# The depthwise convolution's fourth feature block goes from 16 to 31 taps on the tensor engine

## The chip, the cores and the metric

The kernel runs on one core of a Trainium2 chip. What counts is the device time of one execution in microseconds (us), the median of several runs. The engines are told by the profile's names: PE (tensor engine, matmul), PEld (its weight loads), DVE (vector engine), ACT (scalar engine), POOL (GpSimd), SP (the engine whose queue issues the weight loads from memory).

## The reference, cut to what matters

The program is two small networks one after the other on 256 tokens of 1024 features. The first network's second layer has a mixer with a depthwise convolution of 31 taps over 768 features, and that alone is touched here:

```python
def odd_mixer(y, w_in, conv_w, conv_b, cnorm_g, pool_w, pool_scale, w_out):
    z = y @ w_in
    ga, gb, q = jnp.split(z, [D_CONV, 2 * D_CONV], axis=-1)
    u = ga * jax.nn.sigmoid(gb)
    u = lax.conv_general_dilated(u, conv_w[:, None, :], window_strides=(1,),
                                 padding=[(CONV_WIDTH // 2, CONV_WIDTH // 2)],
                                 dimension_numbers=('NWC', 'WIO', 'NWC'),
                                 feature_group_count=D_CONV) + conv_b
    u = jax.nn.silu(rmsnorm(u, cnorm_g))
    ...
    return jnp.concatenate([u, p], axis=-1) @ w_out
```

Around it stand gated feed-forward layers (`half_ffn`: gate and up products into 2816 features, then a down product back), each ahead of and behind the mixer.

## The kernel before

Activations lie with features on the 128 partitions and the 256 tokens along the row. Every large product is made of three half-precision matmuls for each 128x128 tile of weights (`mm3`: high part by high part, high by low, low by high), which PE works through at one 128x256 matmul in about 0.11 us.

**The weights.** Each weight unit (up to 128 x 2048 values) is loaded by SP's queue into one of three staging buffers (`_load`, L122), then split into a high and a low half-precision tile: ACT writes the high part (L137) and DVE the low part (L138), 1024 columns at a time. There are four split buffers, and a unit is split when PE has done with an older one. A staging buffer comes free when DVE has split it, and only then is the next load issued.

**The feed-forward layer ahead of the mixer** (`half_ffn(W, 1, 0, 3, ...)` in `middle`) ends with its down product in `project`: four blocks of 256 features, each of three weight units (8, 8 and 6 tiles of 128 rows). After each block `accumulate` updates the two row blocks of the residual on DVE (L1226), squares them on ACT into one of two buffers of the tag `sq` (L323), and POOL adds the squares together (L311). Ahead of the last block stands a small product on an unsplit weight unit that is read straight from its staging buffer (`early`, matmuls `m<-stage,craw`); that unit is the first of the mixer, `in_o_w_in`.

**The convolution** works on six blocks of 128 features. `CONV` gives for each block the number of taps done by PE, and the engine of the rest: block 0 has all taps on ACT (products, L1390) and POOL (sums, L1391), blocks 1 and 2 all taps on DVE (L1383 for the first, L1385 for the rest), block 3 has 16 taps on PE and 15 on DVE, and blocks 4 and 5 have all 31 on PE. A tap on PE is three matmuls against diagonal 128x128 matrices. `taps`, called between the two feed-forward layers, has POOL build these matrices in advance, two for each tap (high and low part), each with one instruction (L1299). In the program's text they stand ahead of the whole feed-forward layer in whose time they are built.

**After the convolution** `odd` squares the six results on ACT in the order of `ORDER` and sums them over the partitions with a matmul by ones (`m<-sq,ones`), takes the reciprocal root (L333, L334), scales and applies silu (`prep`, L1401, L1402), and feeds the output product `part`. The parts of that product that don't depend on the convolution (kt 6 and 7, the pooling branch) are queued ahead. The next layer's early product (`before`, again `m<-stage,craw`, then a product on POOL in place, L444, and a copy on DVE, L442) stands between.

The order of instructions on each engine is set when the program is built: of the instructions that its own estimate holds to be ready, the one that stands first in the program's text goes first. On the chip each engine then runs its list strictly in that order.

```python
            for i in range(2):
                for k in range(n):
                    nc.gpsimd.tensor_scalar(diag[f][:, i, k], id16, w[:, i, k : k + 1], None, op0=OP.mult)
...
            if n == 31:
                nc.scalar.activation(acc[f], bc[f][:, :S], AF.Identity, scale=ISW, bias=self.v("o_conv_b", f, 1))
...
            if n:
                nc.vector.scalar_tensor_tensor(acc[f], bc[f][:, :S], ISW, acc[f], op0=OP.mult, op1=OP.add)
        add = self.summed(stat[:, :S], direct=6, n=6, ones=ones)
        for f in self.ORDER:
            add(self.square(acc[f], S))
```

Of the kernel before, what the change touches and what calls it, by code (L numbers as in the profile page):

```python
# [215 lines left out]
class Program:  # L216
# [1055 lines left out]
        return rst  # L1272


    CONV = ((0, "gpsimd"), (0, "vector"), (0, "vector"), (16, "vector"), (31, None), (31, None))
    ORDER = (0, 1, 4, 3, 2, 5)

    def taps(self, op, cr):

# [8 lines left out]
        diag = {}  # L1288
        for f, (n, _) in enumerate(self.CONV):
            if n == 0:  # L1290
# [11 lines left out]
    def odd(self, W, y, rst, op, taps):  # L1302
# [18 lines left out]
        for f in range(6):  # L1321
# [15 lines left out]
            nc.vector.scalar_tensor_tensor(up[:, f, 15 : 15 + S], bk[:, :S], ISW, sg, op0=OP.mult, op1=OP.mult)  # L1337
            if self.CONV[f][0]:
                us[f] = t([P, S + 30], f"uh{f}", F16), t([P, S + 30], f"ul{f}", F16)
# [10 lines left out]
        def conv(f, bank):  # L1350
            n = self.CONV[f][0]
            bc[f] = self.bank(bank)
            for k in range(n):
                self.mm3(bc[f][:, :S], diag[f][:, 0, k], diag[f][:, 1, k], us[f][0][:, k : k + S], us[f][1][:, k : k + S], k == 0, k == n - 1)
            if n == 31:
                nc.scalar.activation(acc[f], bc[f][:, :S], AF.Identity, scale=ISW, bias=self.v("o_conv_b", f, 1))
# [21 lines left out]
        nextu = self.before(W, 1, 6, 5)  # L1378
        for f, (n, eng) in enumerate(self.CONV):
            if n == 31:  # L1380
# [13 lines left out]
# [3 lines that stand above are left out]
# [510 lines left out]
```

## Time and profile before

| what | us |
|---|---|
| median of 3 runs | 2735.67 (2726.55 to 2736.68) |
| the profiled execution | 2735.91 |
| its span in the trace | 2734.1 |
| PE busy in the span | 2619.9 (96%) |
| DVE busy in the span | 1749.9 (64%) |

The profiled execution took 1.8 us more than its span; that lies around the span and isn't seen in the trace. Times in the rows below are microseconds from the span's start. In a timeline a row is one or several like instructions: start, length, engine, line, operation, output<-inputs with their shapes, and in brackets how long the engine stood idle before it and what it then waited for.

### The profile page before, as it was taken

How to read it: one execution, taken by the hardware profiler on the slowest of the kernel's cores; microseconds unless marked ns; L12 is line 12 of the kernel's file. 1: busy time of each engine (PE TensorE's matmuls, PEld its weight loads, DVE VectorE, ACT ScalarE, POOL GpSimd, SP SyncE). 2: the span in 40 equal slices, each digit the busy share in tenths (PEclk: the TensorE clock that was granted, in tenths of full speed). 3: DMA queues.
4: the chain of work that ended last, by engine and by line, in shares of the span. 5: the costliest groups of instructions: out<-in, count | busy, mean ns of one | idle time of the engine just before them, and what ended most of it. 6: DMA issues, size and time to landing. Idle time of an engine off the chain costs nothing.

```text
span 2734.1 us, 53369 instructions
## 1 busy us (share of the span) xinstructions
PE 2619.9 (96%) x23012; PEld 2009.6 (74%) x23012; DVE 1749.9 (64%) x2601; ACT 1278.9 (47%) x1821; POOL 423.5 (15%) x413
## 2 busy tenths in 40 slices
PE   8999998799999899999989999999999999999998
PEld 4444444476667678888878887888888888888887
DVE  6676676765567366665676556666565666766664
ACT  5454555443344254444645445554544455544443
POOL 0000010321121000199520010000120300000301
PEclk9999999988798899999999999999999999999999
DMA  9676784100102156655626666555656655556563
GB/s 313 240 254 229 263 291 134 53 27 21 32 14 74 40 171 193 208 184 192 182 79 201 193 194 194 169 177 165 214 170 193 200 163 166 171 157 222 170 193 101
DMA packets 427775, 451.71 MB, mean 165 GB/s; under 512 B 9890, under 2 KB 414920, under 8 KB 420243
## 3 DMA queue, kind: packets, MB, share of 16 engines
q1 hardware_dynamic: 422272, 441.29, 50.7%
q10 hardware_dynamic: 5267, 7.01, 0.8%
q8 instruction: 180, 2.95, 0.5%
q14 instruction: 56, 0.46, 0.1%
HBM read 447.18 MB, written 1.08 MB: 164 GB/s over the span
## 4 chain that ended last, share of the span: by engine, by line
PE 60%; DVE 8%; issue 4%; ACT 4%; DMA 2%; POOL 2%; ACTq 0%; SPq 0%; POOLq 0%; DVEq 0%
PE g L232 48%; PE w L232 4%; PE m L232 4%; DVE w L138 3%; PE n L232 2%; ACT w L137 2%; PE m L235 1%; DVE acc L1385 1%; DMA stage<-in_w_in 1%; DVE SC L1057 1%; POOL acc L1391 0%; DMA stage<-in_o_w_in 0%; PE o L232 0%; DVE yl L347 0%; DVE xn L484 0%
## 5 line engine op out<-in xcount | busy, mean ns | idle before, releaser
L232 PEld LDWEIGHTS <-w 128*128 128x128 f16 x14784 | 1440.5, 98 | 447.2 <-issue 96.9
L138 DVE SCALAR_TENSOR_TENSOR w<-stage,w 128x1024 f16<-128x1024 f32 (+2 forms) x812 | 971.6, 1230 | 455.5 <-ACT w L137 453.2
L137 ACT ACTIVATE w<-stage 128x1024 f16<-128x1024 f32 (+2 forms) x812 | 797.7, 1031 | 542.2 <-PE g L232 317.4
L232 PE MATMUL g<-yh,w 128*128 128x256 f16 x5568 | 931.1, 273 | 8.4 <-ACT yh L346 8.3
L232 PE MATMUL g<-yl,w 128*128 128x256 f16 x2784 | 759.1, 273 | 5.6 <-DVE yl L347 5.1
L232 PE MATMUL g<-hh,w 128*128 128x256 f16 (+1 forms) x1936 | 343.0, 282 | 0.0
L232 PE MATMUL g<-hl,w 128*128 128x256 f16 (+1 forms) x968 | 273.4, 282 | 0.0
L232 PE MATMUL g<-y0h,w 128*128 128x512 f16 (+1 forms) x704 | 219.2, 380 | 8.8 <-ACT y0h L346 8.5
L1299 POOL TENSOR_SCALAR diag<-ident,cws 128x128 f16<-128x128 f16 x156 | 144.2, 943 | 8.9 <-DVE cws L1294 8.9
L232 PE MATMUL g<-w,yh 128*128 128x256 f16 (+1 forms) x928 | 138.1, 262 | 0.2 <-ACT ak L1633 0.2
L232 PE MATMUL g<-y0l,w 128*128 128x512 f16 (+1 forms) x352 | 133.8, 381 | 1.3 <-DVE y0l L347 1.3
L232 PE MATMUL g<-w,yl 128*128 128x256 f16 (+1 forms) x464 | 116.5, 262 | 0.0
L311 POOL TENSOR_TENSOR acc<-sq,sq 128x256 f32<-128x256 f32 (+1 forms) x9 | 11.7, 1295 | 625.4 <-ACT sq L753 338.5
L232 PE MATMUL n<-y0h,w 128*128 128x512 f16 x352 | 108.2, 379 | 0.0
L514 ACT ACTIVATE silu<-g 128x512 f32<-128x512 f32 x50 | 29.9, 597 | 155.9 <-issue 135.0
L232 PEld LDWEIGHTS <-yh 128*128 128x128 f16 x928 | 86.9, 98 | 9.4 <-issue 0.9
L232 PE MATMUL g<-ybh,w 128*128 128x256 f16 x512 | 85.2, 273 | 0.0
L516 DVE SCALAR_TENSOR_TENSOR hid<-g,silu 128x512 f32<-128x512 f32 x55 | 38.0, 691 | 68.9 <-PE g L232 64.5
L311 POOL TENSOR_TENSOR acc<-acc,sq 128x256 f32<-128x256 f32 (+1 forms) x45 | 53.9, 1197 | 156.5 <-ACT sq L753 87.4
L1758 POOL TENSOR_TENSOR rst<-rst,epsgn 128x1 f32<-128x1 f32 x16 | 3.0, 189 | 481.4 <-DVE rst L1757 481.4
L232 PE MATMUL g<-ybl,w 128*128 128x256 f16 x256 | 69.8, 273 | 0.0
L311 POOL TENSOR_TENSOR acc<-Hl 128x256 f32<-128x256 f32 x4 | 2.9, 728 | 427.6 <-DVE Hl L1466 427.6
(408 smaller groups left out, 3108.6 us busy)
## 6 DMA issues: line engine op xcount, KB each, us to landing
stage<-in_ffn_w_gu SPq DMA_DIRECT2D x87, 1024.0 KB
stage<-in_ada_w SPq DMA_DIRECT2D x64, 1024.0 KB
stage<-in_w_in SPq DMA_DIRECT2D x64, 1024.0 KB
stage<-in_ffn_w_down SPq DMA_DIRECT2D x32, 1024.0 KB
stage<-in_w_in SPq DMA_DIRECT2D x54, 512.0 KB
stage<-in_w_ffn_gate SPq DMA_DIRECT2D x22, 1024.0 KB
stage<-in_w_ffn_up SPq DMA_DIRECT2D x22, 1024.0 KB
stage<-in_w_ret_proj SPq DMA_DIRECT2D x16, 1024.0 KB
```

The costliest lines, as they stand in the source:

```text
L137: self.nc.scalar.activation(u.t16[:, 0, c], u.stage[:, c], AF.Copy, scale=SW)
L138: self.nc.vector.scalar_tensor_tensor(u.t16[:, 1, c], u.stage[:, c], SW, u.t16[:, 0, c], op0=OP.mult, op1=OP.subtract)
L232: self.nc.tensor.matmul(out, lhsT, rhs, start=start, stop=stop, skip_group_check=True)
L235: self.nc.tensor.matmul(out, in_, self.ident[:k, :k], start=True, stop=True, is_transpose=True, skip_group_check=True)
L311: self.nc.gpsimd.tensor_tensor(acc, state["x"], x, op=OP.add)
L514: nc.scalar.activation(sg, bg, AF.Silu, scale=ISW)
L516: nc.vector.scalar_tensor_tensor(h, bu, ISW, sg, op0=OP.mult, op1=OP.mult)
L1057: nc.vector.transpose(square(h, g), N[quarter(h, g), :, 16 - 16 * g : 48 - 16 * g])
L1299: nc.gpsimd.tensor_scalar(diag[f][:, i, k], id16, w[:, i, k : k + 1], None, op0=OP.mult)
L1385: nc.vector.scalar_tensor_tensor(acc[f], up[:, f, k : k + S], cw[:, f, k : k + 1], acc[f], op0=OP.mult, op1=OP.add)
L1758: nc.gpsimd.tensor_tensor(st[:, 7:8], st[:, 7:8], self.epsgn, op=OP.add)
```

## The change

Block 3 gets all its 31 taps on PE, as blocks 4 and 5 have them, and none on DVE; and the squares are taken in another order, in which block 3 comes second.

```diff
-    CONV = ((0, "gpsimd"), (0, "vector"), (0, "vector"), (16, "vector"), (31, None), (31, None))
-    ORDER = (0, 1, 4, 3, 2, 5)
+    CONV = ((0, "gpsimd"), (0, "vector"), (0, "vector"), (31, None), (31, None), (31, None))
+    ORDER = (0, 3, 1, 4, 2, 5)
```

Everything else follows from these two lines. `taps` builds 2 x 31 diagonal matrices for block 3 in place of 2 x 16. `conv(3, "m")` issues 93 matmuls in place of 48, and its sum is taken out of the matmul's bank by ACT right away (the branch `n == 31`). The loop over the taps skips block 3, so one L1383, 14 L1385 and the joining L1393 instruction leave DVE.

## Rows read from the trace of the kernel before

**Rows 1.** Page, part 1: busy us, share of the span, instructions, by engine.
```profile
PE 2619.9 (96%) x23012; PEld 2009.6 (74%) x23012; DVE 1749.9 (64%) x2601; ACT 1278.9 (47%) x1821; POOL 423.5 (15%) x413
```

**Rows 2.** Timeline of PE, end of the convolution to the first part after silu.
```profile
1398.30 1.08 PE L232 MATMUL s<-pT,poolw 64*64 64x256 f32 x8
1399.31 1.07 PE L232 MATMUL m<-stage,craw 128*32 128x256 f32 x16
1408.80 1.01 PE L232 MATMUL m<-sel,sq 128*128 128x2 f32 x4 [8.42 <-DVE sq L442]
...
1422.32 0.49 PE L232 MATMUL g<-mixh,w 128*128 128x256 f16 x3 [2.28 <-ACT mixh L339]
```

**Rows 3.** Timeline of DVE, end of the convolution.
```profile
1394.55 13.30 DVE L1385 SCALAR_TENSOR_TENSOR acc<-upad,convw,acc 128x256 f32<-128x256 f32 x24
1407.96 0.42 DVE L1393 SCALAR_TENSOR_TENSOR acc<-m,acc 128x256 f32<-128x256 f32 x1
1408.33 0.42 DVE L442 COPY sq<-m 128x256 f32<-128x256 f32 x1
```

**Rows 4.** Timeline of ACT, 1398 to 1409.
```profile
1398.41 0.47 ACT L1356 ACTIVATE acc<-g,vec 128x256 f32<-128x256 f32 x1 [9.93 <-PE g L232]
1408.31 0.84 ACT L1376 ACTIVATE sg<-s,vec 128x256 f32<-128x256 f32 x2 [9.43 <-DVE acc L1385]
```

**Rows 5.** Windows: busy (count) by engine, then granted clock, DMA share, GB/s.
```profile
1413.00:1414.00 1.00, 1.00 (x7) 0.71 (x5) 0.00 (x0) 0.27 (x1) 0.00 (x0) 0.50 0.03 2
1414.00:1415.00 1.00, 1.00 (x9) 0.83 (x8) 0.00 (x0) 0.00 (x0) 0.00 (x0) 0.86 0.00 0
```

**Rows 6.** Timeline of POOL, 1140 to 1450: start, length, instructions.
```profile
1160.09 144.23 POOL L1299 TENSOR_SCALAR diag<-ident,cws 128x128 f16<-128x128 f16 x156 [8.89 <-DVE cws L1294]
1304.29 0.72 POOL L311 TENSOR_TENSOR acc<-sq,sq 128x256 f32<-128x256 f32 x1
...
1400.49 5.51 POOL L444 TENSOR_TENSOR stage<-stage,gs 128x2048 f32<-128x2048 f32 x1 [24.31 <-PE m L232]
```

**Rows 7.** Timeline of ACT, 1262 to 1345.
```profile
1284.57 0.71 ACT L323 ACTIVATE sq<-Hl 128x256 f32<-128x256 f32 x2
...
1298.06 1.06 ACT L137 ACTIVATE w<-stage 128x1024 f16<-128x1024 f32 x1 [2.35 <-issue]
1305.04 0.72 ACT L323 ACTIVATE sq<-Hl 128x256 f32<-128x256 f32 x2 [5.92 <-POOL acc L311]
1305.67 4.45 ACT L137 ACTIVATE w<-stage 128x1024 f16<-128x1024 f32 x5
```

**Rows 8.** Timeline of DVE, 1299 to 1316.
```profile
1306.74 5.41 DVE L138 SCALAR_TENSOR_TENSOR w<-stage,w 128x1024 f16<-128x1024 f32 x5 [6.37 <-ACT w L137]
1312.42 0.88 DVE L1226 SCALAR_TENSOR_TENSOR Hl<-g,gate,Hl 128x256 f32<-128x256 f32 x2 [0.27 <-PE g L232]
```

**Rows 9.** Timeline of SP's queue, 1308 to 1309: issues of loads.
```profile
1308.17 0.99 SPq L122 DMA_DIRECT2D stage<-in_o_w_in  x2
```

**Rows 10.** Timeline of PE, 1312 to 1315.3.
```profile
1312.11 0.27 PE L232 MATMUL g<-hh,w 128*128 128x256 f16 x1
1314.25 1.07 PE L232 MATMUL m<-stage,craw 128*32 128x256 f32 x16 [1.86 <-DMA stage<-in_o_w_in]
```

**Rows 11.** Tile diag: count, ns minimum/median/maximum, first and last start, form.
```profile
L1299 POOL TENSOR_SCALAR diag<-ident,cws x156: 595/599/2656, 1160.1 to 1303.7; 128x128 f16<-128x128 f16 x156
```

**Rows 12.** Windows as in rows 5 (PE, PEld, DVE, ACT, POOL), another stretch.
```profile
1330.00:1340.00 10.00, 9.69 (x50) 7.81 (x50) 8.55 (x15) 8.29 (x13) 2.60 (x2) 1.00 0.79 245
```

**Rows 13.** Windows, PE on tile diag: length, busy (count), clock, DMA share, GB/s.
```profile
1370.50:1375.75 5.25, 5.23 (x48) 1.00 0.15 51
1388.00:1398.30 10.30, 10.30 (x93) 1.00 0.30 101
```

**Rows 14.** Chain that ended last, in order of time, 1393 to 1425.
```profile
1402.57 3.72 DVE acc L1385
...
1407.36 0.50 DVE acc L1385
```

## The prediction

> **What bounds the kernel now.** I read the page first: PE is busy for 96% of the span [rows 1], so a change pays only where PE stands still, and a delay costs only where it makes PE stand still. The timelines of PE show two such places near the change. The later one is where the taps stand. PE ends the convolution and the matmuls behind it at 1400.38 and then waits 8.42 us, until DVE's copy L442 [rows 2]. That copy is queued behind DVE's taps: 24 taps in 13.30 us, the joining instruction to 1408.38, then the copy [rows 3]. ACT is held as well: it evicts block 5 at 1398.41 and does nothing more until 1408.31 [rows 4]. So DVE's taps set the end of the convolution. PE then resumes at half its clock: 0.50 in the microsecond from 1413, 0.86 in the next, so full from about 1414.3 [rows 5].
>
> The earlier place lies 100 us ahead. POOL builds the diagonals without a pause from 1160.09 to 1304.32 and only then does its first sum of squares [rows 6]. The squares for that sum were ready at 1285.3; ACT's next pair, which needs the buffers, waits 5.92 us for that sum and runs at 1305.04, and the weight splits queued behind it run from 1305.67 [rows 7]. DVE had nothing to split from 1300.38 to 1306.74 [rows 8]. The first of its five splits ends at about 1307.96, frees a staging buffer, and SP issues the next load at 1308.17 [rows 9]. PE waits for that very load: it ends the third of the down product's four blocks at 1312.38 and starts again at 1314.25, after 1.86 us of idleness [rows 10]. So POOL's building of diagonals is late already, and PE already feels the end of that chain.
>
> **The change, part by part.**
>
> *More diagonals.* 186 in place of 156, so 30 more POOL instructions, in a stretch in which POOL had no pause. They go ahead of the sums: the program's text has them first, and the trace shows that order kept although the squares lay ready for 19 us. One costs 144.23/156 = 0.925 us in the mean [rows 6], but 0.595 to 0.599 at minimum and median and 2.656 at most [rows 11]: the mean holds waits beside DVE. From 1304.3 on DVE has no split to do, since ACT is blocked; two L1226 are all that comes [rows 8]. I take 30 x 0.598 = 17.9 and 0.3 for these two, 18.2; the bounds are 17.9 and 27.7 (30 x 0.925).
>
> [...]
>
> *What that delays.* The first sum of squares moves from 1304.3 to 1322.5, ACT's next pair to 1323.2, and with it, in the same order and at the same distances, the split (1306.74), the load (1308.17) and PE's restart (1314.25). PE's work ahead of it is not delayed: it went on through ACT's pause up to 1312.4, since four buffers hold the three units of that block already split. So the wait of 1.86 grows to about 20.1 us, and 18.2 of that is new. Nothing later gives it back: loads and splits shift alike, and PE has no pause to lose before the convolution (0.31 us in the ten with the most, of 1320 to 1350 [rows 12]).
>
> *The clock.* After a wait of 8.42 us PE ran at 0.50 from 1408.8 to about 1414.3 [rows 2, 5]: 5.4 us that did the work of 2.7. After a wait of 20 us I expect the same loss, 2.7 (0 to 4; the level of 0.50 is 1.2 GHz, full is 2.4). If PE's restart is not what ends last there, part of it is hidden. The earlier place together: 18.2 + 2.7 = **20.9 later**.
>
> *More matmuls.* 93 in place of 48: 45 more. 93 take 10.30 us less a tail of about 0.1, and 48 take 5.23 [rows 13], so 0.11 each and 4.9 us on PE, all on the path. Block 5 ends at 1403.2 in place of 1398.3 (times here without the shift from the earlier place), and the early matmuls at 1405.3.
>
> *Taps taken from DVE.* 14 of the 24 L1385 [rows 3], the L1383 ahead of them and the L1393 go. The ten taps of block 2 that are left depend on one another and take 0.50 each, as the last ones of the chain do [rows 14], so DVE ends at about 1399.2 in place of 1408.4. The tap of 3.72 us [rows 14] lies beside POOL's product L444 (1400.49, 5.51 us) [rows 6]; that product now comes at 1405.4, with no tap beside it. DVE is then no longer the bound: PE is, and behind it the copy L442 and the pooling branch on ACT, which can start at about 1404.4.
>
> *What PE's wait becomes.* The 8.42 shrinks to 0.7 (the copy's 0.42 and the way to and from it; between 0.4 and 2). As PE hardly pauses, the half clock behind it goes too: 2.7 back. The squares: ACT now frees block 3's bank at once, blocks 0, 3, 1, 4 and 2 are ready before block 5, and their matmuls follow at full clock, so the chain squares, root, silu ends earlier relative to the parts that fill PE meanwhile; the wait of 2.28 before the first part after silu [rows 2] may fall to about 1.5 (0 to 3). An eviction of 0.47 on ACT for block 3 lies in ACT's long pause before block 5 [rows 4] and costs nothing; without that pause it would cost its 0.47. The other order of squares costs nothing by itself. The later place: 8.42 - 0.7 + 2.7 + 0.8 - 4.9 = **6.3 earlier** (4 to 8.4, the latter with no wait left at all).
>
> *Sum.* 20.9 - 6.3 = 14.6 us more. Against the profiled execution of 2735.91 (span 2734.1 and 1.8 around it) this is 2750.5; the median of the runs, 2735.67, is the same within 0.3. With the bounds of single terms, POOL's upper one aside, it is 2744 to 2757.
>
> **The rivals.**
>
> *A. ACT's list is another one (not slower).* The lists are made at build time. If the longer run of diagonals makes the builder put weight splits ahead of the waiting squares on ACT, the staging buffer comes free at about 1300.5 and PE doesn't wait for it. It decides at one point: whether ACT's instruction behind the split of 1298.06 is the square or the second half of that split. Against it: in the trace the square stands first although it was 5.9 us late on the chip [rows 7], so the builder did not see the lateness of 156, and need not see that of 186. With the whole delay of the earlier place gone the time is 2735.9 - 6.3 = 2729.6; if just one unit gets ahead, PE has 48 matmuls x 0.11 = 5.3 us more of work, the 1.86 goes, and some 10 us stay: about 2739.
>
> *B. POOL is as slow as in the mean.* If DVE does find work beside the added diagonals, 27.7 in place of 18.2: 2760. For it speaks the mean of all diagonals [rows 6]; against it that DVE's splits wait for the very ACT that is blocked.
>
> *C. The later place gives nothing.* If the copy, the pooling branch and six squares line up behind block 5 on ACT so that PE waits some 6 us more, the gain is eaten by the 4.9 of matmuls: 2735.9 + 20.9 = 2757.
>
> *D. The taps are all there is.* Without any delay by POOL and with PE's waits in the later place gone altogether it would be 2735.9 - 8.4 = 2727.5, the best that the trace allows.
>
> **How the numbers follow.** The forecast 0.64, A 0.17 (two thirds of it the whole gain), B 0.07, C 0.07, D 0.05. The likeliest case gives 2750.5, its own range is 2744 to 2757. Since A and D lie apart from it, the range that holds 8 in 10 reaches down to them: 2728 to 2761. About 0.5% (13.7 us) is what a measurement of this kernel can tell from no change. The forecast lies just over that bound: I give six tenths of its 0.64 to slower (0.38), all of B and most of C: 0.51. A, D and the rest of the forecast lie within the bound, 0.45. Faster by over 0.5% would need 13.7 us, more than D has; 0.04 for what I don't see.
>
> **What would show it.** In the changed trace: 186 diagonals that end at about 1322 and POOL's first sum of squares right behind; ACT's square waiting some 24 us for POOL; PE's wait for `in_o_w_in` ahead of the down product's last block at about 20 us, and a clock of 0.50 for some 5 us after it. In the later place: 93 matmuls for block 3; DVE done before PE; PE's wait for L442 under 2 us; a clock that stays at 1.00. The forecast is wrong if ACT's list has splits ahead of the square, if the diagonals end before 1315 or after 1330, or if PE still waits over 3 us behind block 5.

## The result and the profile after

The changed kernel takes 2754.82 us in the median of 7 runs (2739.81 to 2756.91), the kernel before 2732.15 (2726.55 to 2736.68): the ratio is 1.0069, 95% interval 1.0053 to 1.0085, or 18.9 us (14.5 to 23.2) more. The two medians lie 22.7 us apart and the means of the runs 17.8; the ratio, which lies between, is used here. The forecast was 2750.5, and that PE would lose more ahead of the last block of the down product than it wins behind the taps.

The profiled execution of the changed kernel is its fastest run, 2739.81 (span 2738.0), and at first sight it shows little of the loss. It reaches the first diagonal at 1144.86, the kernel before at 1160.09, over the same program; where that comes from stands in the last section. So traces are compared here from the start of POOL's first diagonal on, in two stretches. The early one ends at block 3's first matmul on PE (tile diag, first start), the late one goes on from there to the residual's first update behind the mixer (first L1226). Behind the late one the changed kernel's trace takes 1308.5 us and the other 1306.9; in the ten traces of this document it is 1306.9 to 1311.9, in no order that follows the edits.

| us | early | late | both |
|---|---|---|---|
| before | 210.43 | 56.69 | 267.12 |
| changed | 229.25 | 55.35 | 284.60 |
| difference | +18.82 | -1.34 | +17.48 |

The engines of the changed kernel, page part 1 (busy us, share of the span, instructions), stand against [rows 1]: PE has 45 matmuls more, DVE 16 instructions fewer, POOL 30 more.

```profile
PE 2610.3 (95%) x23057; PEld 2003.3 (73%) x23057; DVE 1743.1 (64%) x2585; ACT 1280.1 (47%) x1822; POOL 440.3 (16%) x443
```

**The early stretch.** The timelines of POOL, ACT, DVE and PE in the changed kernel (start, length, instruction, idle time before it and its releaser), against [rows 6], [rows 7], [rows 8] and [rows 10]:

```profile
1144.86 161.59 POOL L1299 TENSOR_SCALAR diag<-ident,cws 128x128 f16<-128x128 f16 x186 [8.81 <-DVE cws L1294]
1306.42 0.72 POOL L311 TENSOR_TENSOR acc<-sq,sq 128x256 f32<-128x256 f32 x1
...
1409.01 3.60 POOL L444 TENSOR_TENSOR stage<-stage,gs 128x2048 f32<-128x2048 f32 x1 [29.21 <-PE m L232]
```

```profile
1282.83 1.06 ACT L137 ACTIVATE w<-stage 128x1024 f16<-128x1024 f32 x1 [2.35 <-issue]
1307.17 0.72 ACT L323 ACTIVATE sq<-Hl 128x256 f32<-128x256 f32 x2 [23.28 <-POOL acc L311]
1307.80 4.40 ACT L137 ACTIVATE w<-stage 128x1024 f16<-128x1024 f32 x5
```

```profile
1308.87 5.41 DVE L138 SCALAR_TENSOR_TENSOR w<-stage,w 128x1024 f16<-128x1024 f32 x5 [23.73 <-ACT w L137]
```

```profile
1316.11 1.93 PE L232 MATMUL m<-stage,craw 128*32 128x256 f32 x16 [18.95 <-DMA stage<-in_o_w_in]
```

The chain is to be read downwards. POOL ends 186 diagonals 161.59 us after its first one, 17.36 later than the 156 before. ACT's squares wait 23.28 us for POOL in place of 5.92; the five splits behind them come late on ACT and on DVE, which stands still for 23.73 us; the load waits for a staging buffer and is issued at 1310.30; PE waits 18.95 us for that load in place of 1.86. Windows (busy and count of PE, PEld, DVE, ACT and POOL, then granted clock, DMA share, GB/s) show the clock behind the wait at its half level, 0.50, which it leaves between 1320 and 1321:

```profile
1316.00:1317.00 1.00, 0.89 (x12) 0.52 (x16) 0.00 (x0) 0.00 (x0) 0.00 (x0) 0.50 1.16 289
...
1320.00:1321.00 1.00, 1.00 (x9) 0.77 (x8) 0.17 (x1) 1.00 (x2) 1.00 (x1) 0.72 1.16 290
```

**The late stretch.** The matmuls of block 3 (tile diag) are there, 62 and 31 in place of 32 and 16; the timeline of DVE shows what has become of the other end, against [rows 3]:

```profile
L232 PE MATMUL m<-uh,diag x62: 271/273/273, 1374.1 to 1384.2; 128*128 128x256 f16 x62
...
L232 PE MATMUL m<-ul,diag x31: 270/272/273, 1374.2 to 1384.1; 128*128 128x256 f16 x31
```

```profile
1397.44 5.69 DVE L1385 SCALAR_TENSOR_TENSOR acc<-upad,convw,acc 128x256 f32<-128x256 f32 x11
1406.96 0.06 DVE L1539 MEMSET epsln<- 128x1 f32 x1 [3.82 <-PE g L232]
...
1408.96 0.42 DVE L442 COPY sq<-m 128x256 f32<-128x256 f32 x1 [1.93 <-PE m L232]
1409.31 3.34 DVE L437 TENSOR_SCALAR craw<-vec 128x8 f32<-128x8 f32 x1
...
1412.70 0.75 DVE L342 TENSOR_TENSOR mixl<-sg,mixh 128x256 f16<-128x256 f32 x2
```

DVE is done with its taps at 1403.13 and then stands idle for 3.82 us until PE is done with block 5. PE's wait for the copy L442 has fallen from 8.42 to 0.55. But right behind it stands a wait that the kernel before did not have, in the timeline of PE, against [rows 2]:

```profile
1409.44 0.61 PE L232 MATMUL m<-sel,sq 128*128 128x2 f32 x4 [0.55 <-DVE sq L442]
...
1410.24 0.27 PE L232 MATMUL s<-mixh,w 128*128 128x256 f16 x1
1413.16 0.37 PE L232 MATMUL g<-mixl,w 128*128 128x256 f16 x1 [2.65 <-DVE mixl L342]
```

PE waits 2.65 us for the low part of the pooling branch (`mixl`). DVE is late with it because L437, ahead of it in DVE's list, took 3.34 us: it started at 1409.31, and POOL's product L444 ran from 1409.01 to 1412.61. In the kernel before, where that product was over at 1406.00, the timeline of DVE has L437 at 0.17 us:

```profile
1408.66 0.17 DVE L437 TENSOR_SCALAR craw<-vec 128x8 f32<-128x8 f32 x1
...
1409.93 0.75 DVE L342 TENSOR_TENSOR mixl<-sg,mixh 128x256 f16<-128x256 f32 x2
```

Then the clock is down again, in windows of the changed kernel:

```profile
1415.00:1416.00 1.00, 1.00 (x6) 0.56 (x4) 0.00 (x0) 0.44 (x2) 0.00 (x0) 0.50 0.00 0
1416.00:1417.00 1.00, 1.00 (x11) 0.86 (x10) 0.00 (x0) 0.00 (x0) 0.00 (x0) 0.93 0.04 2
```

### The profile page after: what moved, and what is told of

It reads as the page before. It is cut to its first block, busy times and chain, and to the rows that moved or that the text cites. A ratio compares the mean times of both kernels' runs of the same rounds, so it can differ in the third digit from the quotient of the medians.

```text
span 2738.0 us, 53474 instructions
## 1 busy us (share of the span) xinstructions
PE 2610.3 (95%) x23057; PEld 2003.3 (73%) x23057; DVE 1743.1 (64%) x2585; ACT 1280.1 (47%) x1822; POOL 440.3 (16%) x443
## 3 DMA queue, kind: packets, MB, share of 16 engines
q8 instruction: 180, 2.95, 0.5%
## 4 chain that ended last, share of the span: by engine, by line
PE 57%; POOL 7%; DVE 7%; issue 4%; ACT 3%; DMA 2%; ACTq 0%; SPq 0%; POOLq 0%; DVEq 0%
PE g L232 45%; POOL diag L1299 6%; PE m L232 4%; PE w L232 4%; DVE w L138 2%; PE n L232 2%; ACT w L137 1%; PE m L235 1%; DVE SC L1057 1%; DMA stage<-in_w_in 1%; PE o L232 0%; DMA stage<-in_ffn_w_gu 0%; PE s L232 0%; POOL Hl L1498 0%; DVE T L1060 0%
## 5 line engine op out<-in xcount | busy, mean ns | idle before, releaser
L1299 POOL TENSOR_SCALAR diag<-ident,cws 128x128 f16<-128x128 f16 x186 | 161.6, 887 | 8.8 <-DVE cws L1294 8.8
```

## The experiments

The theory had two parts. Early: the 30 added diagonals hold back POOL's sum of squares, and with it ACT, the splits, the load and PE. Late: POOL's product meets DVE on the way to the pooling branch's low part, and that takes back most of the gain. The main rival was that the matmuls on PE are the loss. The measures of all runs:

| kernel | ratio to before (95%) | early us | late us | PE's wait for the load | PE's wait for `mixl` |
|---|---|---|---|---|---|
| before | 1 | 210.43 | 56.69 | 1.86 | none |
| changed | 1.0069 (1.0053 to 1.0085) | 229.25 | 55.35 | 18.95 | 2.65 |
| e1, before with 30 spare diagonals | 1.0074 (1.0052 to 1.0096) | 229.85 | 57.22 | 20.15 | none |
| e2, changed without the 30 | 1.0002 (0.9986 to 1.0019) | 212.72 | 58.01 | 2.95 | 2.65 |
| e3, changed, L437 on POOL | 1.0061 (1.0042 to 1.0081) | 229.93 | 57.83 | 20.30 | 2.4 |
| e4, e3 with the 30 on ACT | 0.9985 (0.9969 to 1.0001) | 212.13 | 55.25 | 2.27 | 2.4 |
| e5, changed, product waits | 1.0077 (1.0048 to 1.0106) | 229.22 | 51.39 | 18.9 | none |
| e6, e5 with the 30 on ACT | 0.9991 (0.9977 to 1.0005) | 209.64 | 51.39 | 1.0 | none |
| e7, e5 with 48 on ACT | 0.9981 (0.9969 to 0.9994) | 208.18 | 51.38 | none | none |
| e8, changed, old order of squares | one run | 229.27 | 55.32 | 19.0 | 2.65 |

**e1: only the diagonals.** The kernel before, and behind block 3's loop in `taps`:

```diff
+            if f == 3:
+                spare = op.tile([P, 2, 15, P], F16, name="spare")
+                for i in range(2):
+                    for k in range(15):
+                        nc.gpsimd.tensor_scalar(spare[:, i, k], id16, w[:, i, 16 + k : 17 + k], None, op0=OP.mult)
```

> The kernel before, with 16 taps of block 3 on PE as it was, but POOL also builds 30 spare diagonals that nothing reads. Theory (the time goes where POOL's building of diagonals holds back the sums of squares, ACT's squares, the weight splits and the load that PE waits for): POOL's building grows from 144.2 to about 161.6 us, PE's wait ahead of the down product's last block from 1.86 to about 19 us, the clock falls to 0.50 behind it, and the first matmul of block 3's taps comes 18.8 us later after the first diagonal than in the kernel before (210.4 us there); the rest as before: 18.8 us slower in all, ratio about 1.007. Rival (the 45 matmuls and what they move make the loss): ratio 1.000, PE's wait stays at about 1.9 us.

The ratio is 1.0074, the early stretch 229.85 us, 19.4 over the kernel before. The timelines of POOL, ACT and PE in this kernel show the same chain with not one tap moved:

```profile
1179.95 29.08 POOL L1304 TENSOR_SCALAR spare<-ident,cws 128x128 f16<-128x128 f16 x30
```

```profile
1312.59 0.72 ACT L323 ACTIVATE sq<-Hl 128x256 f32<-128x256 f32 x2 [24.55 <-POOL acc L311]
```

```profile
1321.45 1.94 PE L232 MATMUL m<-stage,craw 128*32 128x256 f32 x16 [20.15 <-DMA stage<-in_o_w_in]
```

So the early loss is in what POOL builds, not in what PE multiplies. The spare instructions themselves took 29.08 us, 0.97 each, since they stood among DVE's splits; what the delay costs is set at the end of POOL's queue, where DVE is still (23.73 us without a split in the changed kernel) and diagonals are short.

**e2: only the taps.** The changed kernel, with

```diff
-                for k in range(n):
+                for k in range(16 if f == 3 else n):
```

in `taps`, and `conv` reading the diagonals of k % 16 for block 3.

> The changed kernel, but POOL builds only 16 of block 3's 31 pairs of diagonals, and the taps from 16 on read those of taps 0 to 14: the output of block 3 is another one, all its 93 matmuls are there. Theory: the wait ahead of the down product's last block is back at about 1.9 us, the taps start 210.4 us after the first diagonal, and what is left is the later place alone, a gain of about 1.3 us against the kernel before (18.8 us lost early and 17.5 us in all in the profiled execution): ratio 0.998 to 1.001. Prediction as it was on record: a gain of 6.3 us, ratio 0.9977. Rival (the taps on PE are what costs): ratio 1.005 or more.

The ratio is 1.0002: with the 30 instructions taken away the loss is gone, though all 93 matmuls are there. The late stretch is 58.01, no gain at all against 56.69, so neither the 1.3 expected of it nor the 6.3 of the prediction came. The wait for `mixl` is there as in the changed kernel, 2.65 us, but the half clock behind it lasts longer. In the changed kernel it is over soon after 1416, three microseconds from the wait's end (1413.16); here, where the wait ends at 1404.03, the windows (columns as above) have it until about 1409.9:

```profile
1408.50:1409.50 1.00, 1.00 (x4) 0.84 (x3) 0.00 (x0) 0.00 (x0) 0.00 (x0) 0.50 0.00 0
1409.50:1411.00 1.50, 1.50 (x8) 1.03 (x7) 0.00 (x0) 1.07 (x3) 0.00 (x0) 0.88 0.00 0
```

That is 1.4 of the 2.7 us by which this stretch is longer than in the changed kernel. The other 1.3 lie behind PE's next wait, for `mixh`: PE runs at half clock there too for about 3 us, where neither the kernel before ([rows 2], 0.49 us for the same three matmuls) nor the changed one does, though the wait is 2.28 us in all three. The timeline of PE in e2:

```profile
1416.84 0.80 PE L232 MATMUL g<-mixh,w 128*128 128x256 f16 x3 [2.28 <-ACT mixh L339]
```

So in the late stretch, where e2 has the same instructions as the changed kernel, one trace gains 1.34 us and the other loses 1.3. What decides the length of the half clock is not shown.

The early stretch stayed 2.3 over the kernel before. POOL took 145.42 for its 156, 1.2 more, PE waited 2.95 in place of 1.86, and this time the sixteen early matmuls behind the wait ran at half speed (1.93 us; 1.07 in [rows 10]):

```profile
1307.50 1.93 PE L232 MATMUL m<-stage,craw 128*32 128x256 f32 x16 [2.95 <-DMA stage<-in_o_w_in]
```

**e3: the long instruction taken away from DVE.** The changed kernel, with L437 of that one call on POOL:

```diff
-                nc.vector.tensor_scalar(self.craw[:, :, i], v, SW, None, op0=OP.mult)
+                (nc.gpsimd if on_pool else nc.vector).tensor_scalar(self.craw[:, :, i], v, SW, None, op0=OP.mult)
```

> The changed kernel, but the two small products that scale the vectors for the layer after next (L437) run on POOL, behind its product L444, in place of DVE. Theory for the later place (L437 on DVE meets POOL's product, takes 3.34 us in place of 0.17, holds the pooling branch's low part behind it, PE waits 2.65 us for that and falls to half clock): the wait and the drop of the clock go, about 2.65 + 1.5 = 4 us faster than the changed kernel, so about 14 us slower than the kernel before, ratio 1.005. Rival (PE would wait there anyway, for ACT's share of the pooling branch or for the squares): PE's wait stays over 2 us and the time is that of the changed kernel, ratio 1.007.

The theory fell in this form. PE's wait for `mixl` is still 2.4 us and the late stretch no shorter (57.83, with a half clock of some 6 us and, as in e2, a second one behind the wait for `mixh`). The timelines of DVE and POOL in this kernel show why:

```profile
1411.36 3.06 DVE L342 TENSOR_TENSOR mixl<-sg,mixh 128x256 f16<-128x256 f32 x2
```

```profile
1410.20 3.60 POOL L444 TENSOR_TENSOR stage<-stage,gs 128x2048 f32<-128x2048 f32 x1 [29.20 <-PE m L232]
```

With L437 away, `mixl` itself (0.75 for the two in the kernel before) is held until POOL's product is over. L437 was only the first in the queue. The cause is the product, and the remedy is to move that one. The Trainium skill (SBUF — State Buffer, section "Who interferes with whom") has both kinds of victim: a DVE instruction with two SBUF inputs, as `mixl`, contends with a GpSimd instruction that reads SBUF, and a `tensor_scalar`, as L437, can contend where its operands allow a mode with two ports. The traces agree as far as the 3.34 and 3.06 us beside a product of 3.60 go; in which mode L437 ran, no run shows.

**e4: the added diagonals on ACT.** The changed kernel with e3's edit and the following, where `sooner(-LATER)` makes an instruction count as if it stood later in the program's text:

```diff
+                    if f == 3 and k >= 16:
+                        with self.sooner(-LATER):
+                            nc.scalar.activation(diag[f][:, i, k], id16, AF.Copy, scale=w[:, i, k : k + 1])
+                        continue
                     nc.gpsimd.tensor_scalar(diag[f][:, i, k], id16, w[:, i, k : k + 1], None, op0=OP.mult)
```

> The changed kernel with the vectors on POOL as in the run before, and with the 30 added diagonals built by ACT in its pauses in place of POOL; nothing is left out. Theory: both losses go. POOL's building is back at 144 us, PE's wait ahead of the down product's last block at about 1.9 us, no wait for the low part and no half clock behind the taps: 5 us faster than the kernel before, ratio 0.998, if ACT's 30 instructions fit in its pauses at no cost; up to 3 us worse if they hold back the layer's first splits. Rival (POOL is not the cause): ratio 1.005 or more.

The early loss is gone but for 1.7 us with nothing left out (212.13), and the ratio is 0.9985, its interval just reaching 1. The late gain stayed at 1.4 us in place of the whole that was expected: the wait for `mixl` was not repaired, as in e3.

**e5: the product waits.** The changed kernel; the scale of POOL's product is made by a small DVE instruction that reads the low part with factor 0:

```diff
-        nextu = self.before(W, 1, 6, 5)
+        nextu = self.before(W, 1, 6, 5, behind=mix[1][:, 7, 0:KD])
...
+            scale = self.small.tile([P, KD], F32, name=self.name("gs"))
+            self.nc.vector.scalar_tensor_tensor(scale, behind, 0.0, self.gs, op0=OP.mult, op1=OP.add)
```

> The changed kernel; POOL's product L444 behind the taps is made to start only when DVE has written the pooling branch's low part (its scale is taken from a small DVE instruction that reads that part). Theory (POOL's product blocks whichever DVE instruction comes next, L437 in the changed kernel and the low part itself where L437 was taken away): L437 is back at 0.17 us, PE's wait of 2.65 us for the low part falls under 0.5 us, the clock stays at 1.00, and from the first tap of block 3 to the first update of the residual it takes about 51.5 us in place of 55.4 (56.7 in the kernel before); the ratio to the kernel before is about 1.0055. Rival (something else would hold PE there, such as the squares or the matmul by ones): the stretch stays over 54.5 us.

The late stretch is 51.39 us, 3.96 less than in the changed kernel and 5.3 less than before, as forecast from the theory. In the timelines of DVE and POOL:

```profile
1415.02 0.17 DVE L437 TENSOR_SCALAR craw<-vec 128x8 f32<-128x8 f32 x1
...
1415.88 0.75 DVE L342 TENSOR_TENSOR mixl<-sg,mixh 128x256 f16<-128x256 f32 x2
```

```profile
1416.97 3.60 POOL L444 TENSOR_TENSOR stage<-stage,gs 128x2048 f32<-128x2048 f32 x1 [31.46 <-DVE gs L1239]
```

Windows of the same kernel (columns as above) have the clock at full where it was at 0.50 in the changed kernel:

```profile
1416.00:1417.00 1.00, 0.87 (x7) 0.64 (x5) 0.80 (x3) 0.22 (x1) 0.03 (x1) 1.00 0.10 28
```

The ratio, 1.0077, does not show the 4 us: its interval, 1.0048 to 1.0106, holds both 1.0055 and the changed kernel's 1.0069. The trace decides here, the time does not.

**e6 and e7: both repairs.** e5 with the 30 added diagonals on ACT as in e4 (e6, with a LATER of 1200 in place of 2600), and with 48 of the 186 there (`k >= 7`, e7).

> The changed kernel with both repairs and nothing left out: the 30 added diagonals on ACT, POOL's product behind the low part. Theory: from the first diagonal to block 3's first tap 212 us as in the run with the diagonals on ACT (210.4 before), from there 51.5 us (56.7 before): 3.5 us faster than the kernel before in the trace from the first diagonal to the first update of the residual, ratio 0.997 to 0.999. Rival (the gain of the later place is given back downstream): ratio 1.000.

> As the run before, but ACT builds 48 of the 186 diagonals and POOL 138, fewer than the 156 of the kernel before. Theory: POOL ends about 17 us earlier, some 128 us after its first diagonal; ACT's squares no longer wait for it, and the wait for the load ahead of the down product's last block, 1.86 us in the kernel before, goes as well: to the first tap about 208 us, 5.5 us faster than the kernel before in all, ratio 0.9965 to 0.9985. Rival (that wait has another cause, the load itself or its queue): PE's wait stays at 1.5 us or more, ratio as in the run before.

e6 gains 6.1 us in the two stretches; its ratio, 0.9991 (0.9977 to 1.0005), just misses the 0.997 to 0.999 expected and does not rule out that nothing changed. e7 gains 7.6 us in the two stretches, 5.5 expected, and is 0.2% faster than the kernel before: 0.9981 (0.9969 to 0.9994). POOL builds 138 diagonals in 129.07 us and waits for ACT again instead of the other way round, in the timeline of POOL:

```profile
1281.98 0.72 POOL L312 TENSOR_TENSOR acc<-sq,sq 128x256 f32<-128x256 f32 x1
1292.40 3.13 POOL L312 TENSOR_TENSOR acc<-acc,sq 128x256 f32<-128x256 f32 x2 [9.70 <-ACT sq L324]
```

PE starts the early matmuls without a wait, at full speed:

```profile
1305.21 1.07 PE L233 MATMUL m<-stage,craw 128*32 128x256 f32 x16
```

So the 1.86 us of [rows 10] were POOL's too, and the rival for them is out. In the late stretch the three kernels in which the product waits (e5, e6, e7) take 51.38 to 51.39 us, the five others with block 3 on PE 55.25 to 58.01.

**e8: the order of the squares.** The changed kernel with the old `ORDER`.

> The changed kernel with the old order of the squares (0, 1, 4, 3, 2, 5). Theory: the order is worth nothing by itself, since the matmuls by ones stand behind the early product and all squares but the last are ready by then: from the first tap of block 3 to the first update of the residual 55.4 us, within 0.5. Rival (the order lets the chain of squares end sooner): over 56 us.

55.32 against 55.35 us: in this one trace that half of the change does nothing in the late stretch.

## Why the prediction was right, and where it was not

*More diagonals and what they delay: right, a little less than forecast.* POOL's end moved by 17.36 us (18.2 in the sum), PE's wait by 17.09, from 1.86 to 18.95 (18.2), and the order on ACT was the one assumed: the square stands ahead of the splits, so rival A did not come true. Rival B is out too: the extra diagonals cost 17.36/30 = 0.58 us each, since DVE did stand still. The sum had 0.598 for each, the length of one instruction, but at the end of the queue in the changed kernel one starts 0.579 us after the other. Its 0.3 for two L1226 was nothing: on DVE they stand behind the five splits, and the first ran at 1314.20, when POOL had been done for 7.8 us. e1 shows the mechanism alone, e2 its absence.

*The clock: right in kind.* PE ran at 0.50 for somewhat over 4 us behind the long wait. From the early matmuls to the residual's matmul `m<-sel` it took 17.5 us (1316.11 to 1333.64), 2.1 more than the 15.4 before; 2.7 was in the sum. Some 0.4 us of this came back ahead of the taps, where the prediction had nothing come back. The early stretch lost 18.82 where 20.9 was forecast.

*More matmuls, fewer taps: right.* The 45 matmuls cost 4.9 us: from block 3's first matmul to the end of the taps it took 32.8 us (1374.11 to 1406.89) in place of 27.8 (1370.52 to 1398.37). DVE ended 3.8 us before PE, and the wait for L442 shrank to 0.55 (0.7).

*What PE's wait becomes: wrong.* The step that failed is "that product now comes at 1405.4, with no tap beside it". It looked only for taps. In the kernel before the product's victim was a tap of 3.72 us [rows 14] near the end of DVE's taps; in the changed kernel the product comes later, as forecast, but just when DVE turns to L437 and `mixl`, and PE needs `mixl` next. 2.65 us of wait and a half clock took back 3.96 us (e5). With 0.55 us for L442 that makes 3.2 us of waiting behind block 5, where the prediction called itself wrong at over 3, and the clock did not stay at 1.00 there. With that out of the way the late gain is 5.3 us, not 6.3: the wait of 2.28 ahead of the first part after silu did not shrink (2.28 in the changed kernel and in e5; 1.5 was in the sum). The sum took the squares to be ready ahead of block 5, so that the chain behind them could end sooner. But ACT's last two squares still wait for PE's own matmuls by ones, 2.10 us in the kernel before and 1.72 in the changed one, and from there to PE's restart it is 6.94 us in both. The timeline of ACT in the changed kernel:

```profile
1417.63 0.85 ACT L323 ACTIVATE sq<-acc 128x256 f32<-128x256 f32 x2 [1.72 <-PE m L232]
```

In the profiled execution of the changed kernel the gain was 1.34, outside the 4 to 8.4 given for this place; with the longer half clock of e2 and e3 there is none.

*The sum.* 20.9 - 6.3 = 14.6 was forecast, 18.82 - 1.34 = 17.48 is in the trace, 18.9 (14.5 to 23.2) in the runs. That it came so near is in part luck: the late place won 5.0 us less than forecast, and the early one lost 2.1 less, which hid some of it. The late place failing put the result between the forecast and rival C (no late gain), but not by the mechanism that C named. The bounds of the single terms, as the prediction has them, add up to 9.5 to 18.2 us more (17.9 + 0 - 8.4 and 18.2 + 4 - 4), so to 2745 to 2754 and not quite to the 2744 to 2757 that it gives. Why the runs show a little more than the two stretches of this one trace is not shown. The longer half clock of e2 and e3 would add 2.5 to 2.7 us in executions that have it, and the 1.6 us behind the late stretch lie within the scatter of the traces.

## What to carry to other kernels

A step that is moved to the tensor engine takes its preparation along: count the instructions that build the new operands, on the engine that builds them, and look at who is queued behind them there and whether that engine is already late. The mean of an instruction type can be the wrong price for added ones (0.925 us in the mean here, 0.58 for the added); what counted is what the other engine does at the end of that queue. And when a POOL instruction moves in time, list every DVE instruction that will then run beside it, not only those that ran beside it before.

## What the runs showed of the hardware that was not expected

The same program up to the first diagonal took 1144.86 us in the profiled execution of the changed kernel and 1160.09 in that of the kernel before, and between these in the other traces (1145.37 in e3, 1158.37 in e6). Up to there both traces have 1260 instructions on DVE, 769 on ACT and 98 on POOL. The windows of the early network in the kernel before, and then in the changed one, differ in the granted clock, 0.80 against 0.93, while PE is about as busy:

```profile
600.00:700.00 100.00, 95.12 (x1233) 65.95 (x1229) 64.40 (x136) 34.89 (x62) 19.51 (x15) 0.80 0.09 27
```

```profile
600.00:700.00 100.00, 93.70 (x1393) 67.16 (x1394) 69.15 (x150) 39.94 (x72) 22.45 (x18) 0.93 0.10 27
```

In the same 100 us PE got through 1393 matmuls in place of 1233. Whatever decides the clock there, a single profiled execution of this kernel is good to 15 us only, as much as the change is worth; the early stretch behind it agrees to 0.7 us between the traces with the same diagonals (229.22 to 229.93), the late one to 0.01 where the clock stays up (51.38 to 51.39).

A short wait can cost as much again as it lasts, and the same wait does not always cost the same. Ahead of the last block PE waited 1.86 us and went on at full clock in the kernel before; it waited 2.95 us in e2 and the sixteen matmuls behind took 1.93 us in place of 1.07. Behind the wait for `mixl`, 2.4 to 2.65 us in five kernels, the half clock lasted about 3 us in the changed kernel, e4 and e8 and about 6 in e2 and e3. In e2 and e3 the wait of 2.28 us for `mixh` was followed by some 3 us of half clock as well, in the eight other traces by none. Together that is the difference between late stretches of 55.3 and of 57.8 to 58.0. Taking the wait for `mixl` away gave back 3.96 us against the shorter of these.
